# Bidirectional SSM states stored block-first, new limits and prices in a hand planner, and three loads and products moved

## The chip, the core and the metric

The program runs on one core of a Trainium2 chip. The core has TensorE (matmuls into PSUM, its weight loads are listed apart as PEld), VectorE (DVE in the profile), ScalarE (ACT), GpSimd (POOL) and SyncE (SP, which here only issues DMAs). Each engine works through its own queue in order. The metric is the device time of one execution in microseconds (us); lower is better.

## The reference

One layer of an encoder, for 256 tokens of 2048 features, all in float32. Shortened:

```python
h = rmsnorm(x, norm_mix_pre)
q_na, k_na, v_na, u_ssm, q_mem = split(h @ w_in)          # 1024,1024,1024,512,512
y_na  = neighbourhood_attention(q_na, k_na, v_na, na_rpb)  # 8 heads of 128
y_ssm = s5_mixer(u_ssm, ...)                               # 32 groups of 16 channels
y_mem = memory_cross_attention(q_mem, mem, ...)            # 4 heads of 128, 256 memory tokens
y = concat(rmsnorm(y_na), rmsnorm(y_ssm), rmsnorm(y_mem))
x = x + rmsnorm(y @ w_out, norm_mix_post)
f = square(relu(rmsnorm(x, norm_mlp_pre) @ w_ff1)) @ w_ff2
x = x + rmsnorm(f, norm_mlp_post)
```

The part that matters here is `s5_mixer`: for each of two directions and 32 groups, a complex diagonal recurrence of 64 states over the tokens, `h[t] = lam_bar * h[t-1] + b_bar @ u[t]`, then `y = Re(c @ h)`, summed over both directions, plus `d*u`, then GELU and a gate.

## The kernel before

**The weights set the pace.** All weight matrices are cut in 128x128 blocks and laid out in the order of use, eight blocks to a chunk `128x1024` (372 loads in all, the first chunk in three pieces). SP loads a chunk into `wraw`; ScalarE rounds it to `wh` (`conv_high`), VectorE makes the rest `wl = wraw - wh` (`conv_low`), and TensorE multiplies in three passes, high by high, high by low and low by high (`mm3`, `mm_tok`), which keeps float32 accuracy at the fast rate. `take` hands out blocks; when a chunk is used up it converts the chunk two ahead (`AHEAD`) and calls `tick`. `wraw`, `wh` and `wl` have three buffers each.

**A planner written by hand.** The order of instructions on each engine is the program's order. Everything beside the weight stream (attention heads, the SSM, norms) is written as generators, `spawn`ed with a priority and the engines that they load (`uses`). Four clocks in `clk` (V, G, A for VectorE, GpSimd, ScalarE, and E for TensorE) are moved on by a price for every instruction issued (`Engine.call`, `book`). `tick` lets a task take its next step if its time has come and if each engine in `uses` is booked ahead of TensorE by less than `BACK`, in ns. Nothing of this runs on the chip: it decides only in which order instructions stand in the queues.

**The SSM.** Tokens are permuted so that a block is four consecutive tokens, 64 blocks (`NB`). `prep_b` builds input weights, `incr` multiplies them with the inputs and ScalarE copies the result into `XS[g]` (two halves g of the states, each 128 partitions x 2 (real, imaginary) x 16 x 64 blocks; the backward direction is written in reverse). `tree` then runs a prefix scan over the 64 blocks in place: six levels up, five down. On a level with distance h it takes every 2h-th block `dst` and the one h before it, `src`, and does `dst += a*src` for complex a in four VectorE instructions of `2*16*n` elements, n being 32, 16, 8, 4, 2, 1 going up and 1, 3, 7, 15, 31 going down. `ssm_out` multiplies the finished states with output weights: 128 matmuls with 32 stationary columns each, four side by side, whose moving operand `h` is one state row of 63 or 64 blocks.

**Loads.** `load_b` fetches the raw SSM input weights; k-th blocks of x come through `x_in`. `before_dma[c]` holds calls to be made just before chunk c is loaded.

**The end of the first half.** The last quarter of the output projection is evacuated, its squares are summed, `rsqrt_pool` takes a power on GpSimd with a refining step on VectorE, `gpost[3]` (norm weights of the last quarter) is multiplied in by GpSimd, and `x1_part` adds the result to x, 128 columns at a time first, so that TensorE can transpose (`h_turn`) and go on with the MLP.

Of the kernel before, what the change touches and what calls it, by code (L numbers as in the profile page):

```python
# [11 lines left out]
F32 = mybir.dt.float32  # L12
# [27 lines left out]
MARGIN1 = 1200.0  # L40
SH_V = 1e9
SH_G = 500.0
BACK_V, BACK_G, BACK_A = 2600.0, 4000.0, 2200.0
WARM0, WARM1 = 7, 10
LAM_BACK = 900.0
GLU_AT = 1
# [55 lines left out]
def hybrid_kernel(ctx: ExitStack, tc: tile.TileContext, A: dict, out: bass.AP, dbg=None):  # L102
# [16 lines left out]
    class Engine:  # L119
# [3 lines left out]
        def __getattr__(self, name):  # L123
            f = getattr(self.raw, name)
            e = self.e

            def call(o, *a, **kw):
                n = 1
                for d in o.shape[1:]:
                    n *= d  # L130
                if e == "E":
                    m = a[0].shape[-1]
                    if name == "transpose":
                        c = 110.0
                    elif a[0].dtype == F32R:
                        c = n * 0.4225
                    else:
                        c = max(n, 128) * 1.69 * (0.31 if m == 32 else 1.0) if n > 4 else 110.0
                elif name == "tensor_reduce":
                    c = 80 + 1.04 * a[0].shape[1] * a[0].shape[2]  # L140
                elif e == "A":
                    c = 100 + 0.83 * n + (95 if any(isinstance(x, bass.AP) for x in kw.values()) else 0)
                elif e == "V":
                    c = (72 if n > 64 else 140) + n * {"tensor_copy": 0.52, "reciprocal": 8.0, "tensor_tensor_scan": 1.04,
                                   "tensor_scalar": 0.76, "memset": 0.3}.get(name, 1.04)
                else:
                    c = 155 + n * {"tensor_scalar": 0.9, "memset": 0.0, "tensor_copy": 1.6}.get(name, 2.1)
                book(e, c)
                return f(o, *a, **kw)  # L149
            return call  # L150
# [17 lines left out]
    def tt(eng, o, a, b, op):  # L168
        eng.tensor_tensor(o, a, b, op=op)
# [10 lines left out]
    def act(o, i, f=AF.Copy, **kw):  # L180
        ACT.activation(o, i, f, **kw)
# [37 lines left out]


    tasks = []
    BACK = dict(V=BACK_V, G=BACK_G, A=BACK_A)

    def spawn(gen, pri=1, uses="VA", after=None):
        i = sum(1 for t in tasks if t[0] <= pri)
        tasks.insert(i, [pri, gen, clk[after] + MARGIN + MARGIN1 if after else clk["E"], uses])
        return gen
# [15 lines left out]
    def tick():  # L243
        for t in list(tasks):
            more = t[2] <= clk["E"]
            while more and all(clk[e] - clk["E"] < BACK[e] for e in t[3]):
                more = step(t)

    def drain(g):
# [179 lines left out]
    def x_in(k0, k1):  # L429
        q = k0 // 8  # L430
        if q not in xst:
            xst[q] = a2.tile([128, 8, 256], F32, name="xst", tag="AB", bufs=2)
        nc.sync.dma_start(xst[q][:, k0 - 8 * q:k1 - 8 * q, :], A["xT"][:, k0:k1, :])

    def m_in(q):
        mst[q] = a1.tile([128, 4, 256], F32, name="mst", tag="xst", bufs=2)
# [214 lines left out]
    def prep_b(ut):  # L651
        yield from until(lambda: ut in loaded and clk["E"] > loaded[ut][1])
        raw = loaded[ut][0]
        w = a2.tile([128, 2, 2, 4, 4, 16], F32, name="W", tag="W", bufs=1)
        par = a2.tile([128, 4, 2, 2, 4], F32, name="par", tag="par", bufs=1)
        for i, x in enumerate((cfr, cfi, lbr, lbi)):
            act(par[:, i], x[:, 8 * ut:8 * ut + 8].rearrange("p (d q) -> p d q", d=2)[:, :, None, :]
                .to_broadcast([128, 2, 2, 4]))
        for l in range(4):
            o = w[:, :, :, :, l, :]  # L660
            src = (w[:, :, :, :, l - 1, :].rearrange("p d c q b -> p (d c q) b") if l
                   else raw.rearrange("p (n b) -> p n b", b=16))
            r_, i_ = (par[:, 2 * min(l, 1) + i].rearrange("p d c q -> p (d c q)")[:, :, None].to_broadcast([128, 16, 16])
                      for i in range(2))
            t = a2.tile([128, 2, 2, 4, 16], F32, name="pt", tag="pt", bufs=1)
            tt(V, t.rearrange("p d c q b -> p (d c q) b"), src, i_, mult)
            tt(V, o.rearrange("p d c q b -> p (d c q) b"), src, r_, mult)
            tt(V, o[:, :, 0], o[:, :, 0], t[:, :, 1], sub)
            tt(V, o[:, :, 1], o[:, :, 1], t[:, :, 0], add)
            yield True  # L670
        yield
        act(W0[ut].rearrange("p d c q j b -> p (d c q) j b"),
            w[:, :, :, :, 0, :].rearrange("p d c q b -> p (d c q) b")[:, :, None, :].to_broadcast([128, 16, 2, 16]))
        w0_done.add(ut)
        if ut % 2 == 0:
            XS[ut // 2] = a2.tile([128, 2, 16, NB], F32, name="XS", tag="AB", bufs=2)
        for d in range(2):
            for j in range(2):
                h = slice(64 * j, 64 * j + 64)
                act(wx[h, :, ::-1 if d == 0 else 1, j, :], w[h, d].rearrange("p c q l b -> p (c q) l b"))  # L680
            yield
            wt = a2.tile([128, 2, 4, 128], F32, name="W1T", tag="W1T", bufs=2)
            for c in range(2):
                p = att()
                for q in range(4):
                    PE.transpose(p[:, q * 128:(q + 1) * 128], wx[:, 4 * c + q].rearrange("p l j b -> p (l j b)"), ident)
                act(wt[:, c].rearrange("p q m -> p (q m)"), p)
            spawn(incr(ut, d, wt), 2, "A")
            yield
        yield from until(lambda: (ut, 1) in xs_part)  # L690

    def incr(ut, d, wt):

        yield from until(lambda: ssm_done and (d == 0 or (ut, 0) in xs_part))
        p = att()
        X = p.rearrange("p (c q m) -> p c q m", c=2, q=4)
        for c in range(2):
            for q in range(4):
                PE.matmul(X[:, c, q, :], wt[:, c, q, :], U4[:, 4 * ut + q, :], start=True, stop=True,
                          skip_group_check=True)  # L700
        c0 = 8 * (ut % 2) + 4 * d
        o = XS[ut // 2][:, :, c0:c0 + 4, :]
        act(o[:, :, :, ::-1] if d else o, X)
        xs_part.add((ut, d))
        yield

# [45 lines left out]
    def tree(g):  # L752

        X = XS[g]
        cols = slice(16 * g, 16 * g + 16)
        for up, l in [(1, l) for l in range(LEV)] + [(0, l) for l in range(LEV - 2, -1, -1)]:
            h = 1 << l
            d0 = 2 * h - 1 if up else 3 * h - 1
            n = len(range(d0, NB, 2 * h))
            dst, src = X[:, :, :, d0::2 * h], X[:, :, :, d0 - h:NB - h:2 * h]  # L760
            t = a2.tile([128, 2, 16, NB // 2], F32, name="ps", tag="ps", bufs=1)[:, :, :, 0:n]
            tt(V, t, src[:, ::-1], pw[:, l, 0:2, cols][:, :, :, None].to_broadcast([128, 2, 16, n]), mult)
            tt(V, dst, dst, t, add)
            tt(V, t, src, pw[:, l, 2, cols][:, None, :, None].to_broadcast([128, 2, 16, n]), mult)
            tt(V, dst, dst, t, add)
            yield True
        yield
# [4 lines left out]
    def ssm_out(ut):  # L772
# [7 lines left out]
        for i in range(4):  # L780
            for d in range(2):
                l = (i + 1) % 4 if d == 0 else (4 - i) % 4
                for c in range(2):
                    for q in range(4):
                        h = H[:, c, 8 * (ut % 2) + 4 * d + q, :]

                        if d == 0:
                            o0, h = (1, h[:, 0:NB - 1]) if l else (0, h)
                        else:
                            o0, h = (0, h[:, NB - 2::-1]) if l else (0, h[:, ::-1])  # L790
                        n = NB - 1 if l else NB
                        PE.matmul(p[32 * q:32 * q + 32, i * NB + o0:i * NB + o0 + n], CC[ut][:, l, c, 4 * d + q, :],
                                  h, start=False, stop=(i == 3 and d == 1 and c == 1), skip_group_check=True,
                                  tile_position=(0, 32 * q))
# [113 lines left out]


    for ut in range(2):  # L910
        load_b(ut)
    spawn(lam_task("V"), 2, "V")
    spawn(b_task(), 3, "VA")
    spawn(c_task(), 3, "VA")
    spawn(k0_task(), 3, "VA")
    spawn(tree_task(), 4, "V")
    st = spawn(ssm_task(), 5, "GA")

    st_rx = {}
# [284 lines left out]
    ts(v1, v1, 1.0 / D, mult, EPS, add)  # L1204
    stt(v1[:, 1:2], sx, 1.0 / D, v1[:, 1:2], mult, add)
    rsqrt_pool(r1, v1)
    for t in range(2):
        a = acc1[:, t, quarter(3)]
        tt(G, a, a, gpost[3], mult)
    B = ExitStack()  # L1210
    bp = B.enter_context(tc.tile_pool(name="bp", bufs=1, side="right"))
    hs = bp.tile([128, KT, 2, 256], F32R, name="hs")
# [38 lines left out]
    x1_part(slice(128, 256))  # L1251
    h_turn(1)
    h_high(1)
    conv_low(first)
    W.nv += 1
    h_low(0)
# [236 lines left out]
```

## Time and profile before

| | us |
|---|---|
| median of 3 runs | 1175.65 (1172.53 to 1177.12) |
| the profiled execution | 1176.17 |
| its span, first to last instruction | 1174.4 |

The span falls into stages: 0 to 58 us the first projections, 58 to 150 memory keys and values, 150 to 336 neighbourhood attention with the SSM's trees beside it, 336 to 440 the output projection, 440 to 454 the norm between the halves, and from 454 the MLP, in which TensorE is never idle until 1150. In a row of the timeline stand start, duration, engine, line, operation, `out<-in`, shapes, count, and in brackets how long the engine was idle before it and who ended that. Since one helper issues nearly all instructions, all have line 149 and are told apart by their tiles.

### The profile page before, as it was taken

What the parts mean: (1) busy time and instruction counts of PE and PEld (TensorE: products, weight loads), DVE (VectorE), ACT (ScalarE), POOL (GpSimd) and SP (SyncE); (2) the same over time, 40 slices, a digit from 0 to 9 for tenths busy, and PEclk for the clock granted to TensorE, in tenths of its full rate; (3) what the DMA queues carried; (4) which work ended last, traced back from release to release, by engine and by line L of the source; (5) the groups of instructions that cost most, each with busy time, mean ns of one, the idle gap of its engine ahead of it and who ended that gap; (6) DMA issues with size and microseconds to landing.
All of it is one profiled execution on the core that took longest, in us unless ns stands there. A gap on an engine that the chain in (4) does not pass through costs nothing.

```text
span 1174.4 us, 17404 instructions
## 1 busy us (share of the span) xinstructions
PE 1129.9 (96%) x6776; PEld 976.4 (83%) x6776; DVE 718.5 (61%) x1060; ACT 588.7 (50%) x908; POOL 97.7 (8%) x161
## 2 busy tenths in 40 slices
PE   8989896999989998999999999999999999999996
PEld 7978796989878887888888888888888888888885
DVE  6767498566966766676665444445666665445454
ACT  5677643566455546555455434343444544344342
POOL 1750000010000034000000000000000000011011
PEclk9999998999999999999999999999999999999998
DMA  8875353344444684666666666666666666666673
GB/s 285 303 218 171 109 162 104 100 131 138 154 127 142 187 280 145 182 190 188 195 187 189 186 191 184 191 185 192 189 190 194 186 192 184 193 193 197 189 210 127
DMA packets 62723, 213.05 MB, mean 181 GB/s; under 512 B 7216, under 2 KB 8752, under 8 KB 62640
## 3 DMA queue, kind: packets, MB, share of 16 engines
q1 hardware_dynamic: 62352, 211.84, 58.6%
q8 instruction: 53, 0.87, 0.3%
q14 instruction: 30, 0.25, 0.1%
q10 hardware_dynamic: 288, 0.09, 0.0%
HBM read 209.81 MB, written 2.10 MB: 180 GB/s over the span
## 4 chain that ended last, share of the span: by engine, by line
PE 72%; DVE 3%; issue 1%; ACT 1%; POOL 0%; DVEq 0%; ACTq 0%; POOLq 0%
PE acc L149 66%; PE big L149 5%; PE att L149 2%; DVE wl L149 1%; DVE ps L149 1%; DVE XS L149 1%; POOL x L149 0%; DVE facc L149 0%; ACT CC L149 0%; ACT wh L149 0%; DVE mn L149 0%; DVE rt L149 0%; DVE P L149 0%; DVE r L149 0%; ACT yH L149 0%
## 5 line engine op out<-in xcount | busy, mean ns | idle before, releaser
L149 DVE TENSOR_TENSOR wl<-wraw,wh 128x1024 fp32r<-128x1024 f32 (+1 forms) x372 | 454.2, 1225 | 389.2 <-ACT wh L149 389.0
L149 ACT ACTIVATE wh<-wraw 128x1024 fp32r<-128x1024 f32 (+1 forms) x372 | 391.2, 1054 | 419.4 <-PE acc L149 303.5
L149 PE MATMUL acc<-hs,wh 128*128 128x512 f32 (+1 forms) x996 | 346.4, 391 | 0.0
L149 PE MATMUL acc<-hs,wl 128*128 128x256 f32 x992 | 279.8, 283 | 0.0
L149 PEld LDWEIGHTS acc<-hs,wh 128*128 128x128 f32 x996 | 187.1, 188 | 38.6 <-ACT hs L149 0.2
L149 PEld LDWEIGHTS acc<-hs,wl 128*128 128x128 f32 x992 | 187.9, 190 | 0.0
L149 PE MATMUL acc<-wh,fH 128*128 128x512 f32 x448 | 178.8, 399 | 0.0
L149 PE MATMUL acc<-wh,fL 128*128 128x512 f32 x448 | 176.7, 394 | 0.0
L149 PE MATMUL acc<-wl,fH 128*128 128x512 f32 x448 | 175.7, 392 | 0.0
L149 PEld LDWEIGHTS acc<-wh,fL 128*128 128x128 f32 x448 | 84.1, 188 | 21.8
L149 PEld LDWEIGHTS acc<-wl,fH 128*128 128x128 f32 x448 | 84.1, 188 | 20.1
L149 PEld LDWEIGHTS acc<-wh,fH 128*128 128x128 f32 x448 | 84.1, 188 | 19.2
L149 PE MATMUL acc<-xH,wl 128*128 128x256 f32 x256 | 74.8, 292 | 9.3 <-DVE wl L149 9.2
L149 PE MATMUL acc<-xH,wh 128*128 128x256 f32 x256 | 77.2, 301 | 4.4 <-ACT wh L149 4.4
L149 PE MATMUL acc<-xL,wh 128*128 128x256 f32 x256 | 74.0, 289 | 0.0
L149 PEld LDWEIGHTS acc<-xH,wl 128*128 128x128 f32 x256 | 50.6, 198 | 10.6 <-DVE wl L149 10.6
L149 PEld LDWEIGHTS acc<-xH,wh 128*128 128x128 f32 x256 | 50.8, 199 | 5.2 <-ACT wh L149 4.6
L149 PEld LDWEIGHTS acc<-xL,wh 128*128 128x128 f32 x256 | 50.7, 198 | 0.4
L149 POOL TENSOR_TENSOR facc<-facc,g 128x512 f32<-128x512 f32 x6 | 10.1, 1710 | 475.5 <-DMA g<-in_g_dram 475.5
L149 PE MATMUL acc<-wh,mixn 128*128 128x512 f32 x128 | 40.8, 396 | 0.0
L149 ACT ACTIVATE P<-P,mn 128x256 f32<-128x256 f32 x24 | 12.0, 501 | 40.8 <-DVE mn L149 40.8
L149 DVE TENSOR_TENSOR XS<-XS,ps 128x32 f32<-128x32 f32 (+9 forms) x44 | 29.1, 661 | 1.5
(305 smaller groups left out, 1503.0 us busy)
## 6 DMA issues: line engine op xcount, KB each, us to landing
wraw<-in_w_dram SPq DMA_DIRECT2D x369, 512.0 KB, 4.3
tokst<-in_xt_dram SPq DMA_DIRECT2D x4, 512.0 KB, 7.9
mst<-in_memT_dram SPq DMA_DIRECT2D x4, 512.0 KB, 4.6
tokst<-in_mt_dram SPq DMA_DIRECT2D x4, 512.0 KB, 6.3
bias<-in_bias_dram SPq DMA_DIRECT2D x8, 256.0 KB, 4.0
x<-in_xt_dram SPq DMA_DIRECT2D x8, 256.0 KB, 5.9
out_dram<-facc SPq DMA_DIRECT2D x8, 256.0 KB, 2.4
xst<-in_xT_dram SPq DMA_DIRECT2D x7, 256.0 KB, 7.4
```

Source lines behind the costliest of these rows:

```text
L149: return f(o, *a, **kw)
```

## The change

Five things are edited.

1. `XS` and the tree's scratch `ps` are stored with the block as outer axis and the 2x16 state columns inside. `incr`, `tree` and `ssm_out` index them accordingly; what is computed stays the same.
2. The tree task is let in by a limit of its own, key `v`: VectorE's bookings less than 1700 ns ahead of TensorE, where it was 2600 as for others.
3. ScalarE's price for n elements goes from `100 + 0.83n` (and 95 if any operand beside the input is a tile) to `205 + 0.83n`, plus 80 with a tile as scale or with a bias, plus 186 with an accumulated sum; its limit goes from 2200 to 3800 ns.
4. The loads of the first two blocks of SSM input weights move from the start of SP's queue to just before chunks 5 and 6, and the first block of x is issued by ScalarE's queue in place of SP's.
5. The two GpSimd products with `gpost[3]` stand, in the program, behind the first two transposes and roundings of the next stage.

```diff
-BACK_V, BACK_G, BACK_A = 2600.0, 4000.0, 2200.0
+BACK_V, BACK_G, BACK_A, BACK_TREE = 2600.0, 4000.0, 3800.0, 1700.0
...
-                    c = 100 + 0.83 * n + (95 if any(isinstance(x, bass.AP) for x in kw.values()) else 0)
+                    c = (205 + 0.83 * n + (80 if isinstance(kw.get("scale"), bass.AP) or "bias" in kw else 0)
+                         + (186 if "accum_out" in kw else 0))
...
-    BACK = dict(V=BACK_V, G=BACK_G, A=BACK_A)
+    BACK = dict(V=BACK_V, G=BACK_G, A=BACK_A, v=BACK_TREE)
...
-            while more and all(clk[e] - clk["E"] < BACK[e] for e in t[3]):
+            while more and all(clk[e.upper()] - clk["E"] < BACK[e] for e in t[3]):
...
-        nc.sync.dma_start(xst[q][:, k0 - 8 * q:k1 - 8 * q, :], A["xT"][:, k0:k1, :])
+        (nc.sync if k0 else nc.scalar).dma_start(xst[q][:, k0 - 8 * q:k1 - 8 * q, :], A["xT"][:, k0:k1, :])
...
-            XS[ut // 2] = a2.tile([128, 2, 16, NB], F32, name="XS", tag="AB", bufs=2)
+            XS[ut // 2] = a2.tile([128, NB, 2, 16], F32, name="XS", tag="AB", bufs=2)
...
-        o = XS[ut // 2][:, :, c0:c0 + 4, :]
-        act(o[:, :, :, ::-1] if d else o, X)
+        act(XS[ut // 2][:, ::-1 if d else 1, :, c0:c0 + 4], X.rearrange("p c q m -> p m c q"))
...
-            dst, src = X[:, :, :, d0::2 * h], X[:, :, :, d0 - h:NB - h:2 * h]
-            t = a2.tile([128, 2, 16, NB // 2], F32, name="ps", tag="ps", bufs=1)[:, :, :, 0:n]
-            tt(V, t, src[:, ::-1], pw[:, l, 0:2, cols][:, :, :, None].to_broadcast([128, 2, 16, n]), mult)
+            dst, src = X[:, d0::2 * h], X[:, d0 - h:NB - h:2 * h]
+            t = a2.tile([128, NB // 2, 2, 16], F32, name="ps", tag="ps", bufs=1)[:, 0:n]
+            tt(V, t, src[:, :, ::-1], pw[:, l, 0:2, cols][:, None].to_broadcast([128, n, 2, 16]), mult)
             tt(V, dst, dst, t, add)
-            tt(V, t, src, pw[:, l, 2, cols][:, None, :, None].to_broadcast([128, 2, 16, n]), mult)
+            tt(V, t, src, pw[:, l, 2, cols][:, None, None, :].to_broadcast([128, n, 2, 16]), mult)
             tt(V, dst, dst, t, add)
...
-                        h = H[:, c, 8 * (ut % 2) + 4 * d + q, :]
+                        h = H[:, :, c, 8 * (ut % 2) + 4 * d + q]
...
-        load_b(ut)
+        at(before_dma, 5 + ut, load_b, ut)
...
-    spawn(tree_task(), 4, "V")
+    spawn(tree_task(), 4, "v")
...
     rsqrt_pool(r1, v1)
-    for t in range(2):
-        a = acc1[:, t, quarter(3)]
-        tt(G, a, a, gpost[3], mult)
...
     x1_part(slice(128, 256))
     h_turn(1)
     h_high(1)
+    for t in range(2):
+        a = acc1[:, t, quarter(3)]
+        tt(G, a, a, gpost[3], mult)
     conv_low(first)
```

## The prediction

> **What bounds the kernel now.** I read the page first (TensorE busy, the chain), then busy time by stage, then the list of who waited for whom, then the timeline around each wait of TensorE, and last the groups by form.
>
> ```profile
> PE 1129.9 (96%) x6776; PEld 976.4 (83%) x6776; DVE 718.5 (61%) x1060; ACT 588.7 (50%) x908; POOL 97.7 (8%) x161
> ```
>
> TensorE is busy in 1129.9 of 1174.4 us. A change that leaves its matmuls alone can only win from the 44.5 us in which it is idle, so the question is where these lie. Stages (columns: stretch, its length, then busy us of PE, PEld, DVE, ACT, POOL):
>
> ```profile
> 58.00:150.00 92.00, 84.57 (x549) 72.40 (x548) 60.69 (x125) 64.92 (x126) 17.56 (x53) 0.98 0.53 160
> 150.00:200.00 50.00, 39.59 (x300) 37.92 (x299) 48.33 (x73) 23.10 (x39) 0.73 (x1) 0.92 0.41 127
> 285.00:336.00 51.00, 45.54 (x328) 43.01 (x325) 49.10 (x69) 22.12 (x42) 0.74 (x1) 0.97 0.44 146
> 440.00:454.00 14.00, 10.46 (x60) 8.88 (x60) 10.83 (x17) 8.16 (x15) 8.56 (x7) 0.88 0.34 108
> ```
>
> The reader is to see the second and third row: 10.4 and 5.5 us of TensorE idle, and VectorE at 48.3 of 50 and 49.1 of 51 us. These are the two prefix trees of the SSM (one per half of the states). There VectorE is the bound: TensorE needs `wl`, the low half of each weight chunk, from the same VectorE queue. Its waits, one by one (in brackets the idle time before and who ended it):
>
> ```profile
> 156.49 0.38 PE L149 MATMUL acc<-xH,wl 128*128 128x256 f32 x1 [1.11 <-DVE wl L149]
> 177.96 0.32 PE L149 MATMUL att<-U,W1T 128*128 128x64 f32 x1 [1.31 <-ACT W1T L149]
> 193.84 0.58 PE L149 MATMUL acc<-xH,wh 128*128 128x256 f32 x1 [4.36 <-ACT wh L149]
> 198.27 0.58 PE L149 MATMUL acc<-xH,wl 128*128 128x256 f32 x1 [3.64 <-DVE wl L149]
> 317.39 0.39 PE L149 MATMUL acc<-xH,wl 128*128 128x256 f32 x1 [0.93 <-DVE wl L149]
> 325.15 0.54 PE L149 MATMUL acc<-xH,wl 128*128 128x256 f32 x1 [3.33 <-DVE wl L149]
> 333.52 0.50 PE L149 MATMUL acc<-wl,mixm 128*128 128x512 f32 x1 [0.93 <-DVE wl L149]
> ```
>
> The 4.36 us at 193.84 are put down to ScalarE, but ScalarE was busy in only 23 of these 50 us: its queue stood behind a softmax step that waited for VectorE. So 8.0 us at the end of tree one and 5.2 us in tree two are VectorE's backlog.
>
> **The tree's layout.** Level l of a tree takes every 2·2^l-th block. In the old layout the block is the innermost axis, so elements lie 8 bytes apart on level 0, 16 and more above. Groups of VectorE by form, 150 to 345 us (count, busy us, mean ns):
>
> ```profile
> L149 DVE TENSOR_TENSOR qk<-acc,rb_x 128x512 f32<-128x512 f32 x8 | 5.5, 688 | 0.2 <-PE acc L149 0.2
> L149 DVE TENSOR_TENSOR XS<-XS,ps 128x1024 f32<-128x1024 f32 x4 | 4.9, 1226 | 0.1
> L149 DVE TENSOR_TENSOR XS<-XS,ps 128x512 f32<-128x512 f32 x4 | 4.4, 1107 | 0.1
> L149 DVE TENSOR_TENSOR ps<-XS,pw 128x512 f32<-128x512 f32 x4 | 4.3, 1084 | 0.1
> L149 DVE TENSOR_TENSOR XS<-XS,ps 128x480 f32<-128x480 f32 x4 | 4.2, 1045 | 0.1
> L149 DVE TENSOR_TENSOR ps<-XS,pw 128x480 f32<-128x480 f32 x4 | 4.1, 1028 | 0.1
> L149 DVE TENSOR_TENSOR XS<-XS,ps 128x256 f32<-128x256 f32 x4 | 2.6, 658 | 0.1
> L149 DVE TENSOR_TENSOR ps<-XS,pw 128x256 f32<-128x256 f32 x4 | 2.6, 645 | 0.1
> L149 DVE TENSOR_TENSOR W<-W,par 128x256 f32<-128x256 f32 x6 | 2.5, 418 | 0.0
> L149 DVE TENSOR_TENSOR XS<-XS,ps 128x224 f32<-128x224 f32 x4 | 2.4, 588 | 0.1
> L149 DVE TENSOR_TENSOR ps<-XS,pw 128x224 f32<-128x224 f32 x4 | 2.3, 576 | 0.1
> ```
>
> A contiguous 512 takes 688 ns and a contiguous 256 takes 418; the tree's take 1107 and 658. The 1024 (8-byte steps) costs nothing extra. In the new layout the innermost 32 (or twice 16) lie together on every level, so I give each form the contiguous time: 688; 654 for 480 and 384 for 224, on the line through 256 and 512; 418. Saved over both trees, four instructions of each row: (1107+1084-2·688)·4 = 3.26, (1045+1028-2·654)·4 = 3.06, (658+645-2·418)·4 = 1.87, (588+576-2·384)·4 = 1.58, in all 9.8 us; forms of 128 and fewer at nothing. That is **4.9 us for each tree**. In tree one all of it falls in VectorE's unbroken run that ends in the 8.0 us of waits, so TensorE gets 4.9. In tree two the waits come step by step, and what has been saved ahead of each covers all but 0.3 us of the 5.2: 4.9 again. What is late next is the rest: 3.1 us at the end of tree one, and the 1.31 us on ScalarE.
>
> The planner's own price for VectorE (72 ns and 1.04 per element, 604 for 512) does not change; it was 0.5 us short of each strided 512, which is how it let in more stages than VectorE could carry, and is nearly right for contiguous ones. The lower backlog limit (1700 for 2600 ns) holds a stage back by at most 0.9 us. Behind it wait only the SSM outputs; in front go the `wl`. It could win up to the 3.1 us left; below, a later second tree could lose as much as it is held back, 0.9. I take 0.
>
> **Readers and writers of the states.** ScalarE's eight evacuations (512 elements) now read PSUM 256 bytes apart and write runs of four. No row shows ScalarE so; by VectorE's extra of (1107-688)/512 = 0.8 to (658-418)/256 = 0.9 ns per element they cost 0 to 8·512·0.9 = 3.7 us of an engine with half its time free. I take 0, because ScalarE ends only 1.31 us of waits here. The four `ssm_out` blocks read their moving operand 128 bytes apart instead of contiguously:
>
> ```profile
> 219.56 1.97 PE L149 MATMUL att<-XS,CC 128*32 128x63 f32 x128
> 164.89 0.28 PE L149 MATMUL acc<-xH,wh 128*128 128x256 f32 x1
> 165.01 0.28 PE L149 MATMUL acc<-xL,wh 128*128 128x256 f32 x1
> ```
>
> 128 matmuls in 1.97 us, less some 0.2 for the last one's drain, are 32 groups of four column tiles at 55 ns, 0.86 ns per column. Elsewhere TensorE takes 256 columns of 4 bytes each 0.12 us, 0.47 ns per column. So a tile here reads at little over half the rate it can; a halving by the stride would just be hidden. Bounds: 0, and 0.9 ns for every column of 128 groups, 128·64·0.9 = 7.4 us. I take 0, nearest to the 0.47 row. The Trainium skill (Advanced Engine Details and Errata, section Memory Cachelines) speaks against the change: SBUF lines have 16 bytes and two hits on each are needed for full speed, PSUM's have 8. VectorE's rows agree (8-byte steps free, 16-byte steps not); no run yet shows it for TensorE, and by that rule the 7.4 us would be lost.
>
> **ScalarE's prices.**
>
> ```profile
> L149 ACT ACTIVATE U<-uT 32x256 f32<-32x256 f32 x16 | 6.6, 414 | 0.2
> 136.28 0.33 PE L149 MATMUL att<-CC,W 128*32 128x96 f32 x5 [2.53 <-issue]
> 265.59 0.31 PE L149 MATMUL att<-CC,W 128*32 128x96 f32 x4 [2.35 <-ACT CC L149]
> ```
>
> A copy of 256 was booked at 100+0.83·256 = 312 ns and takes 414; now 417 is booked. So steps that TensorE takes up behind ScalarE were put in its queue too early: both `CC` waits above. Right prices could win both, 2.53+2.35 = 4.9 us. Against that the limit rises from 2200 ns, seven such copies or 2.9 us real, to 3800, nine or 3.7: a queue up to 0.8 us deeper ahead of a `wh`. That bites where ScalarE is fullest, from 58 to 150 us (64.9 of 92). TensorE's idle time there, 92-84.6 = 7.4 us, is 4.9 without the first `CC` wait; as the upper end I let it double. No row tells which of the two wins, and they are alike in size: I take 0 and keep -4.9 and +4.9.
>
> **The start.**
>
> ```profile
> 0.72 0.86 SPq L648 DMA_DIRECT2D W<-in_b_dram  x2
> 1.63 0.42 SPq L433 DMA_DIRECT2D xst<-in_xT_dram  x1
> 2.49 0.35 ACTq L197 DMA_DIRECT2D lam<-in_lam_dram  x1
> 4.86 0.51 ACT L149 ACTIVATE xH<-xst,vecs 128x256 fp32r<-128x256 f32 x1 [2.17 <-DMA xst<-in_xT_dram]
> 26.41 0.38 PE L149 MATMUL big<-xH,wh 128*128 128x256 f32 x1 [0.42 <-ACT wh L149]
> ```
>
> Three issues leave the head of SP's queue (the weights follow at about 1.63+0.42 = 2.05, so they start 1.3 us earlier, at 0.72). But the first `xT` block now stands behind `lam` in ScalarE's queue: issued at 2.49+0.35 = 2.84, not 1.63, so `xH` starts 1.2 us later, and TensorE with it. Neither lasts: at 26.41 TensorE waits for weights that come through a DMA queue with the same bytes ahead of them, the two SSM loads now before chunks 5 and 6. Those loads are needed only after GpSimd's lambda chain. I take 0, between -1.3 and +1.2.
>
> **The last norm weights.**
>
> ```profile
> 441.24 0.16 DVE L149 TENSOR_TENSOR rt<-ry 128x2 f32<-128x2 f32 x1 [0.84 <-POOL ry L149]
> 441.31 2.48 POOL L149 TENSOR_TENSOR acc<-acc,gpost 128x512 f32<-128x512 f32 x2
> 441.44 1.15 DVE L149 SCALAR_TENSOR_TENSOR rt<-rt,v 128x2 f32<-128x2 f32 x1
> 442.62 1.19 DVE L149 SCALAR_TENSOR_TENSOR r<-rt,ry 128x2 f32<-128x2 f32 x1
> 444.25 0.33 PE L149 MATMUL att<-ident,x 128*128 128x128 f32 x1 [2.94 <-DVE x L149]
> ```
>
> Two 2-element steps take 1.15 and 1.19 us instead of 0.16, each until one of GpSimd's two products ends; TensorE waits behind them. Moving the products out of the way would win 2.0 us. But between the old and new place in the program lie no GpSimd instructions and nothing that writes what the products read: GpSimd still takes them up right after its power at 441.3. I take 0; -2.0 if the new place adds a wait that holds them, and up to +2.5 (their length) if they then hold back `wl`.
>
> **Sum.** 1176.2 (span 1174.4 and 1.8 around it) - 4.9 - 4.9 = **1166.4 us**. The profiled execution lies 0.5 above the median 1175.65, so this counts as 0.8% faster than before. About 0.5%, 5.9 us, is what a measurement of this kernel tells from no change: faster means under 1169.8, slower over 1181.5.
>
> **Rivals.**
> 1. What I left at 0 comes too: both `CC` waits (-4.9) or one of them with the norm weights (-2.4-2.0): about 1161.7. For it: the waits are there and their cause is a price. Against: the unmoved place in GpSimd's queue. Chance 0.18.
> 2. Strided moving reads cost VectorE's 0.9 ns per column: +7.4, 1173.8. For it: the same step costs VectorE that much. Against: the 0.47 row. Chance 0.15. (The Trainium skill's Memory Cachelines, above, give this one.)
> 3. ScalarE's deeper queue becomes the wait: up to +4.9, 1171.3, astride the border. For it: ScalarE's 71% in that stage. Against: its prices are now right. Chance 0.15.
> 4. Slower: in `ssm_out` the four tiles of a group now read four neighbouring floats at a time. If such reads are served one after another, a group takes 4·55 = 220 ns, 165 more; 128·165 ns = +21.1, 1187.5. The gain is eaten from 9.8 us/128 = 77 ns more (132 ns a group), and the time is slower from 15.1 us/128 = 118 ns more (173 ns a group). Against: the four tiles run side by side now. Chance 0.08.
> 5. The change does not do what it says: patterns with runs of 16 cost VectorE what strides did, 1176. Chance 0.04.
>
> Forecast: 0.40. Faster: forecast, rival 1 and half of 3, 0.65; same: 2, 5, half of 3, 0.27; slower: 4, 0.08. The range goes from rival 1 with some start gain, 1158, to rival 5, 1177; it leaves out rival 4 and the edge of 1.
>
> **What would show it.** Right: tree forms of 512 near 688 ns; TensorE idle in the two tree stretches down to about 5.5 and 0.6; `ssm_out` blocks still 1.97 us; the two 2-element steps at 441 still over 1 us. Wrong: `ssm_out` at 3.8 us or 7 us; new waits for `wh` between 60 and 100 us; TensorE's first weights matmul far beyond 7 us with 26.41 shifted as well.

## The result, and the profile after

| | us | ratio to the kernel before |
|---|---|---|
| before, median in the same comparison | 1176.11 | |
| changed, median of 6 | 1181.87 | 1.0053 (95%: 1.0033 to 1.0074) |
| changed, profiled execution | 1182.86 (span 1181.1) | |

The change makes the kernel slower by half a per cent, about 6.2 us. The prediction, 1166.4 with a range up to 1177, is wrong, in the sign too. The engines' line on the page of the changed kernel:

```profile
PE 1145.4 (97%) x6776; PEld 991.5 (84%) x6776; DVE 709.8 (60%) x1060; ACT 588.6 (50%) x908; POOL 98.4 (8%) x161
```

TensorE is idle for 1181.1 - 1145.4 = 35.7 us, 8.8 less than before; VectorE has 8.7 us less to do. So far this is what was forecast. But the same 6776 matmuls now keep TensorE busy for 15.5 us more. The stages of the changed kernel (stretch, length, busy us of PE, PEld, DVE, ACT, POOL, then the granted clock, DMA share, GB/s):

```profile
58.00:150.00 92.00, 89.86 (x604) 78.20 (x603) 61.69 (x124) 70.14 (x136) 19.77 (x57) 1.00 0.58 178
150.00:200.00 50.00, 45.62 (x336) 43.82 (x335) 42.14 (x85) 27.93 (x56) 1.49 (x2) 0.93 0.42 129
285.00:336.00 51.00, 47.77 (x330) 44.31 (x330) 42.57 (x70) 22.22 (x42) 2.14 (x2) 0.97 0.55 166
440.00:454.00 14.00, 11.00 (x69) 9.71 (x68) 9.44 (x19) 6.22 (x17) 9.23 (x9) 0.92 0.47 154
```

VectorE is no longer full in the tree stretches (42 of 50 us), and TensorE's idle time there falls from 10.4 to 4.4 and from 5.5 to 3.2; from 58 to 150 us it falls from 7.4 to 2.1. The tree itself, VectorE's groups by form from 150 to 345 us in the changed kernel (count, busy us, mean ns):

```profile
L150 DVE TENSOR_TENSOR XS<-XS,ps 128x512 f32<-128x512 f32 x4 | 3.2, 805 | 0.1
L150 DVE TENSOR_TENSOR ps<-XS,pw 128x512 f32<-128x512 f32 x4 | 2.7, 686 | 0.1
L150 DVE TENSOR_TENSOR ps<-XS,pw 128x480 f32<-128x480 f32 x4 | 2.6, 654 | 0.1
L150 DVE TENSOR_TENSOR XS<-XS,ps 128x256 f32<-128x256 f32 x4 | 1.7, 426 | 0.1
L150 DVE TENSOR_TENSOR ps<-XS,pw 128x224 f32<-128x224 f32 x4 | 1.5, 386 | 0.1
```

These are the contiguous prices but for the first row. Three of its four take 0.69 us like the others; the fourth takes 1.14, beside an instruction of GpSimd:

```profile
168.17 0.73 POOL L150 TENSOR_TENSOR sum_mo<-sum_mo,sq 128x256 f32<-128x256 f32 x1 [88.07 <-ACT sq L150]
168.30 1.14 DVE L150 TENSOR_TENSOR XS<-XS,ps 128x512 f32<-128x512 f32 x1
```

Now the reader of the states, TensorE's group of the four `ssm_out` blocks in the stretch from 200 to 380 us, first in the kernel before, then in the changed one:

```profile
L149 PE MATMUL att<-XS,CC 128*32 128x63 f32 (+1 forms) x512 | 7.9, 219 | 0.0
```

```profile
L150 PE MATMUL att<-XS,CC 128*32 128x63 f32 (+1 forms) x512 | 21.0, 348 | 0.0
```

13.1 of the 15.5 us are here. A block takes 5.14 to 5.41 us where it took 1.97, the third for instance:

```profile
339.68 5.14 PE L150 MATMUL att<-XS,CC 128*32 128x63 f32 x128
```

The start, a timeline of the changed kernel (start, duration, engine, line, operation, in brackets the idle time before and who ended it):

```profile
2.88 0.45 ACTq L434 DMA_DIRECT2D xst<-in_xT_dram  x1
9.35 0.51 ACT L150 ACTIVATE xH<-xst,vecs 128x256 fp32r<-128x256 f32 x1 [6.66 <-DMA xst<-in_xT_dram]
10.21 0.58 PE L150 MATMUL big<-xH,wh 128*128 128x256 f32 x1 [4.36 <-ACT wh L150]
11.74 0.33 SPq L300 DMA_DIRECT2D wraw<-in_w_dram  x1
```

The first block of `xT`, issued at 2.88, is used only at 9.35, and TensorE's first weights matmul stands at 10.21. The next chunk is asked for only at 11.74 (7.66 in the kernel before), when a buffer comes free: the weight stream itself is late. And waits of TensorE, from the same trace. The kernel before doesn't have them; only the third, right behind the second tree, has a counterpart there, of 0.93:

```profile
184.21 0.95 PE L150 MATMUL att<-ident,P 128*128 128x128 f32 x4 [2.74 <-ACT P L150]
216.63 3.67 PE L150 MATMUL att<-U,W1T 128*128 128x64 f32 x16 [2.95 <-ACT W1T L150]
328.32 0.50 PE L150 MATMUL acc<-wl,mixm 128*128 128x512 f32 x1 [2.41 <-DVE wl L150]
378.03 0.49 PE L150 MATMUL acc<-wh,mixn 128*128 128x512 f32 x1 [2.10 <-ACT wh L150]
```

So three things have to be told apart: what the strided reads cost and why, what the late start costs, and what the planner's edits win or lose. Experiments are given as ratios to the kernel before on the same chip; a ratio of 0.001 is 1.2 us.

### The profile page after: what moved, and what is told of

The parts are those of the page before. It is cut to its first block, busy times and chain, and to the rows that moved or that the text cites. A ratio compares the mean times of both kernels' runs of the same rounds, so it can differ in the third digit from the quotient of the medians.

```text
span 1181.1 us, 17405 instructions
## 1 busy us (share of the span) xinstructions
PE 1145.4 (97%) x6776; PEld 991.5 (84%) x6776; DVE 709.8 (60%) x1060; ACT 588.6 (50%) x908; POOL 98.4 (8%) x161
## 4 chain that ended last, share of the span: by engine, by line
PE 84%; DVE 4%; ACT 4%; issue 3%; POOL 3%; DMA 2%; DVEq 0%; SPq 0%; ACTq 0%; POOLq 0%
PE acc L150 73%; PE att L150 6%; PE big L150 5%; DVE wl L150 2%; ACT wh L150 1%; DMA wraw<-in_w_dram 1%; DVE ps L150 1%; DMA xst<-in_xT_dram 1%; ACT P L150 0%; POOL cs L150 0%; POOL u L150 0%; POOL x L150 0%; DVE XS L150 0%; POOL t L150 0%; DVE rt L150 0%
## 5 line engine op out<-in xcount | busy, mean ns | idle before, releaser
L150 PEld LDWEIGHTS acc<-wh,mixn 128*128 128x128 f32 x128 | 24.7, 193 | 8.3 <-ACT wh L150 2.5
L150 DVE SCALAR_TENSOR_TENSOR ff<-fr 128x256 f32<-128x256 f32 x64 | 27.2, 425 | 2.2
```

## Which reads are slow

Three probes take the changed kernel and let each of the four blocks read other places of the state tile. `o` is the first element of tile q (four tiles run side by side), `st` the step from column to column, in floats. What the blocks read is no longer what the layer needs, so only the rows of the blocks are used, not the time of these runs. The expectations count a block from its first to its last start; a row of the timeline is 0.2 to 0.4 us longer, by the last matmul's own time.

**Probe 1.** Steps of 4, 8, 16 and 128 bytes, tiles apart.

```diff
-                        h = H[:, :, c, 8 * (ut % 2) + 4 * d + q]
+                        X = H.rearrange("p m c s -> p (m c s)")
+                        o, st = [(64 * q, 1), (128 * q, 2), (256 * q, 4), (4 * q, 32)][ut]
+                        h = X[:, o:o + (NB - 1) * st + 1:st]
```

> The changed kernel, but the four output blocks read other places of the state tile (so the SSM's output is not the layer's): block 1 steps of 4 bytes, block 2 steps of 8, block 3 steps of 16 with the four column tiles 1 KB apart, block 4 steps of 128 with the four tiles 16 bytes apart. Unchanged they take about 5.0 us each, 1.97 before the change. Theory A, a moving read pays for each new 16-byte line: blocks 1 and 2 take 1.97, blocks 3 and 4 some 3.8 to 5.0. Theory B, the cost comes from four tiles reading one line at once: blocks 3 and 4 take 1.97 too. Theory C, any step but 1 is slow: block 1 alone is fast.

The four blocks in its timeline, in this order:

```profile
227.31 1.99 PE L150 MATMUL att<-XS,CC 128*32 128x63 f32 x128
241.78 2.12 PE L150 MATMUL att<-XS,CC 128*32 128x63 f32 x128
332.96 3.96 PE L150 MATMUL att<-XS,CC 128*32 128x63 f32 x128
349.64 3.71 PE L150 MATMUL att<-XS,CC 128*32 128x63 f32 x128
```

Steps of 8 bytes are nearly free, steps of 16 bytes double the block. The last block has the changed kernel's step of 128 bytes, but its four tiles lie 16 bytes apart instead of 4, and it takes 3.71, not 5.2. So there are two costs, one of the step and one of where the tiles lie.

**Probe 2.** `o, st = [(512 * q, 8), (512 * q, 3), (q, 4), (0, 32)][ut]`: 32 and 12 bytes with tiles 2 KB apart, 16 bytes on neighbouring floats, and 128 bytes with all four tiles on the same floats.

> The changed kernel, whose four blocks of C H read other places of the state tile, so that the output isn't the reference's. In the earlier probe a block took 1.77 us with steps of 4 bytes, 1.90 with 8, 3.66 with 16 and tiles 1 KB apart, 3.43 with 128 and tiles 16 bytes apart, against 4.8 to 5.2 in the changed kernel (128 bytes, tiles 4 bytes apart). Now: steps of 32 bytes and tiles 2 KB apart; 12 bytes, 2 KB apart; 16 bytes, tiles 4 bytes apart; 128 bytes, all four tiles at the same address. If a column that lies on a new group of 16 bytes costs double: 3.4 to 3.7; 2.8 to 3.3 (three of four columns are on a new one); and if four tiles on one group wait for each other, 4.8 to 5.2 for the third and the fourth. If only different tiles on a power of two wait for each other: 3.5 and 1.8 to 2.0 for the first two. If tiles that ask for the same address are served at once: 3.4 to 3.7 for the fourth.

```profile
225.97 4.03 PE L150 MATMUL att<-XS,CC 128*32 128x63 f32 x128
242.48 3.02 PE L150 MATMUL att<-XS,CC 128*32 128x63 f32 x128
334.92 3.96 PE L150 MATMUL att<-XS,CC 128*32 128x63 f32 x128
351.60 5.75 PE L150 MATMUL att<-XS,CC 128*32 128x63 f32 x128
```

The first two came close to what the first theory had. With steps of 12 bytes three of four columns begin in a new group of 16 bytes, with 8 bytes one of two, from 16 bytes on every one, and start to start the blocks take 2.77, 1.90 and 3.66 to 3.73: about 3.7 us times that share, and never under 1.8. The third was expected at 4.8 to 5.2 and is 3.66: four tiles on one group of 16 bytes do not wait for each other by that alone. The fourth (5.39) excludes that equal addresses are served at once.

**Probe 3** tells what is left: long steps on a shared group, or that all columns of all tiles lie at one place of a period of 128 bytes. `o, st = [(q, 20), (q, 16), ((q // 2) * 4 + q % 2, 32), (q, 28)][ut]`: 80, 64, 128 and 112 bytes; on neighbouring floats but for the third, where two tiles lie in one group and two in the next.

> The changed kernel, whose four blocks of C H read other places of the state tile, so that the output isn't the reference's: steps of 80 bytes, tiles 4 bytes apart; 64 bytes, tiles 4 bytes apart; 128 bytes, two tiles on one group of 16 bytes and two on the next; 112 bytes, tiles 4 bytes apart. If the last third of the cost comes from all columns lying at the same place of a period of 128 bytes: 3.4 to 3.8; more than that, 3.8 to 5 (two places of the period); 3.4 to 4.5; 3.4 to 3.8. If it comes from long steps on a shared group: 4.8 to 5.4 for the first and the last, too. If the period is 64 bytes: 3.4 to 3.8, 4.8 to 5.4, 3.4 to 4.5, 3.4 to 3.8.

```profile
224.69 4.21 PE L150 MATMUL att<-XS,CC 128*32 128x63 f32 x128
241.38 4.02 PE L150 MATMUL att<-XS,CC 128*32 128x63 f32 x128
334.49 4.13 PE L150 MATMUL att<-XS,CC 128*32 128x63 f32 x128
351.33 3.94 PE L150 MATMUL att<-XS,CC 128*32 128x63 f32 x128
```

All four are back at the doubled time (start to start 3.91, 3.72, 3.84 and 3.64; the first is a little over what was expected, the second a little under). Long steps on a shared group (the first and the last) aren't the cause, nor is a period of 64 bytes (the second). Two places of 128 bytes (the second, the third) are enough to take the extra away. Only where every read of all four tiles falls on one place of a 128-byte period, as in the changed kernel, does a block take over 5 us. Only steps of 128 bytes show it here; longer ones were not tried, and what part of the memory that place is, the runs don't say.

So the changed kernel pays twice: about 2.0 us per block for the step (3.96 for 1.99), 8.0 in all, and about 1.3 for the shared place (5.14 to 5.41 for 4.0), 5.1 in all, together the 13.1 us of the two group rows.

## What each part is worth

**The layout alone** (the kernel before with the `XS`, `ps`, `incr`, `tree` and `ssm_out` lines of the diff).

> The kernel before with the new layout of states and scratch alone. Theory A (the strided reads of the output blocks cost 3.2 us each, 12.7 in all, and the trees win their 9.8 or less): 1176.1 + 12.7 - 9.8 = 1179 or somewhat more, with four output blocks of 5 us. Rival (the loss sits in the start and in the planner's new order, and the long output blocks only fill time in which TensorE would have waited): 1166 to 1172.

Ratio 1.0017 (1.0005 to 1.003). Its blocks take 5.23 to 5.55 us, and TensorE's idle time in the two tree stretches is 5.66 and 2.77: what the tree wins, the reads take.

**Everything but the layout** (the changed kernel with the old layout).

> The changed kernel with the old layout, everything else of the change kept. Theory A: output blocks back at 1.97 us (-12.7), the trees slow again (at most +9.8), so 1181.9 - 12.7 + 5 to 9.8 = 1174 to 1179. Rival (the loss sits in start and order): 1182 or more, since the trees' gain is lost as well.

Ratio 0.9995 (0.9984 to 1.0006). The other edits together are worth nothing, although their waits for `P`, `W1T` and at the output projection are all there. The parts don't add up: on the new layout the same edits cost 1.0053 - 1.0017 = 0.0036, 4.2 us (some 2.8 either way).

**Another layout: real and imaginary part innermost.** TensorE then steps 8 bytes, and VectorE reads pairs. First on the changed kernel (`incr` and `tree` index the tile accordingly):

```diff
-            XS[ut // 2] = a2.tile([128, NB, 2, 16], F32, name="XS", tag="AB", bufs=2)
+            XS[ut // 2] = a2.tile([128, 16, NB, 2], F32, name="XS", tag="AB", bufs=2)
...
-                        h = H[:, :, c, 8 * (ut % 2) + 4 * d + q]
+                        h = H[:, 8 * (ut % 2) + 4 * d + q, :, c]
```

> The changed kernel with a third layout: 16 state columns outside, then the block, then the real and imaginary part innermost. The output blocks read in steps of 8 bytes, and the trees take pairs of 8 bytes that lie 16 bytes and more apart. Theory A: output blocks 1.97 us, tree forms of 512 near 690 ns if two hits on a line are enough, so 1181.9 - 12.7 = 1169; if VectorE pays by the jump and not by the element, about 900 ns for 512 and some 1174. Rival C (any step is slow): output blocks stay at 5 us, 1182.

Ratio 0.9947 (0.9929 to 0.9964), 12.5 us less than the changed kernel (some 3 either way), by this alone. The blocks take 2.11 to 2.13 us.

**The same layout on the kernel before, nothing else changed.**

> The same layout on the kernel before, with nothing else changed: beside the same with GpSimd's norm products really moved, 1167.64. That one shows waits of TensorE for x, released by GpSimd, of 0.92, 4.02 and 0.74 us, where the others have one of 3.0: if the real move costs these 2.7 us, 1164 to 1166; if it costs nothing, 1167 to 1168. By the sum of the layout alone (1.7) and the strided reads (12.7): 1163.5.

Median 1165.41, ratio 0.9926 (0.9911 to 0.9942): faster than both kernels, and near what I had forecast for the change. By its ratio it is the fastest version here; two more below (0.9928 and 0.9935) can't be told from it. Its tree stretches:

```profile
150.00:200.00 50.00, 44.31 (x334) 43.19 (x333) 43.71 (x76) 24.58 (x40) 0.73 (x1) 0.93 0.43 149
285.00:336.00 51.00, 48.17 (x445) 44.59 (x445) 41.07 (x70) 25.92 (x50) 2.90 (x3) 1.00 0.51 164
```

TensorE is idle for 5.7 and 2.8 us of them. A faster tree without slow reads is worth 0.0074, 8.7 us; the slow reads cost 1.0017 - 0.9926 = 0.0091, 10.7 us, with some 2 us of uncertainty beside the 13.1 of the rows.

## The late start

**The changed kernel with the first `xT` load back on SP's queue.**

> The changed kernel with the first xT load back on SP's queue, everything else as changed. In the changed kernel's trace that load is issued on ScalarE's queue at 2.88 us and lands at 9.26, and the first weights matmul stands at 10.21 behind a wait of 4.36 us for wh; its weights matmuls are 4.5 us behind those of the kernel before at the start, 1.8 at 54 us and 1.3 at 73. If the start is caught up later, as I forecast: no wait over 1 us at the first weights matmul, and a time within 0.7 us of the changed kernel's 1181.9. If the delay that is left at 73 us stays to the end: 1.3 to 1.8 us less, 1180.1 to 1180.6. If all of the first wait reaches the end: 4.4 less, 1177.5.

```profile
3.28 0.51 ACT L150 ACTIVATE xH<-xst,vecs 128x256 fp32r<-128x256 f32 x1 [0.59 <-DMA vecs<-in_vecs_dram]
5.51 0.56 PE L150 MATMUL big<-xH,wh 128*128 128x256 f32 x1
```

`xH` starts at 3.28 and the first weights matmul at 5.51, with no wait ahead. Median 1177.93, ratio 1.0025 (1.0015 to 1.0035) where the changed kernel has 1.0053: about 0.0028, 3.3 us, but by the two intervals anything from 0.6 to 6, which leaves room for the last two of the three expectations. The traces are sharper. The first weights matmul lies 4.7 us ahead of the changed kernel's (5.51 and 10.21), the four matmuls on `P` 2.85 (181.36 and 184.21), the matmul behind the wait of 2.10 us 2.65 (375.38 and 378.03), and the first matmul on `x` at the end of the first half 2.65 (448.38 and 451.03). So over half of the delay is never caught up.

**The pair layout on the changed kernel, with the same load back.**

> The changed kernel with real and imaginary part innermost and with the first xT load back on SP's queue. Without the second it has 0.9947 of the kernel before; the same layout on the old planner and loads has 0.9926; the xT load alone was worth 0.0028 on the changed layout (1.0053 to 1.0025). If the load is all that the other edits cost: 0.991 to 0.993, 1163 to 1165. If the planner's edits cost something of their own: 0.994 or more, 1166 and above.

Ratio 0.9935 (0.992 to 0.995), between the two expectations. With the pair layout the planner's and the load edits cost 0.9947 - 0.9926 = 0.0021; the load's part is 0.0012, about half, but these intervals don't tell half from none or all. In the two traces TensorE's first matmul on `x` stands at 434.96 and, with the load back, 432.85.

## The planner's edits

**ScalarE's prices and limit on the kernel before** (with the moved norm products, which change nothing there).

> The kernel before with ScalarE's new prices and its limit of 3800 and with the last norm weights moved: the old layout, the old limit for the tree, the old loads. If ScalarE's edits are what empties the stretch from 58 to 150 us (idle 7.43 before, 2.14 in the changed kernel): its idle time there falls to 2 or 3 us and the time is 1169 to 1172 on a scale where the kernel before has 1174.5. If the waits that came with the changed kernel (P, W1T and wl at 184, 217 and 328 us, and wh and wl at the GLU) are ScalarE's work being priced higher and so let in later: these waits, 2.7, 2.9, 2.4 and 2.9 us, are here too and give the gain back, 1174 to 1178. If they come from the tree's lower limit or the moved loads, none of them is here. The moved norm weights by themselves: 0, as the changed kernel's row of rt and its gap of 3.00 us show.

Ratio 0.9974 (0.9962 to 0.9986). The idle time from 58 to 150 us falls from 7.4 to 2.1, as in the changed kernel, so this edit is what empties that stage. But part comes back; two waits of its trace:

```profile
183.84 1.54 PE L150 MATMUL att<-U,W1T 128*128 128x64 f32 x6 [5.31 <-ACT W1T L150]
367.31 0.79 PE L150 MATMUL acc<-wh,mixn 128*128 128x512 f32 x1 [2.10 <-ACT wh L150]
```

**The layout with the tree's lower limit.**

> The kernel before with the new layout and the tree's lower limit of 1700, and ScalarE's old prices, old loads. Beside it stands the layout alone, 1.7 us over the kernel before (ratio 1.0017). If the lower limit is worth nothing, as I forecast: the same, 1175 to 1177. If it lets the tree in so late that the SSM's output is ready too late for the GLU (2.10 and 0.77 us of waits at 378 us in the changed kernel, and 5 us of delay gathered there): these waits are here and the time is 1179 to 1182. If ScalarE's prices do that: the waits are not here.

Ratio 1.006 (1.0047 to 1.0074), 5 us over the layout alone. My mechanism for it fell: at the output projection there is only a wait of 0.76. The tree begins at 159 us instead of 147, the last step of the second tree starts at 328 instead of 323, and the wait behind it grows. That wait, and the clock after it:

```profile
330.11 0.79 PE L149 MATMUL acc<-wl,mixm 128*128 128x512 f32 x1 [3.39 <-DVE wl L149]
```

```profile
330.00:332.00 2.00, 1.89 (x5) 1.51 (x6) 2.00 (x4) 0.00 (x0) 0.00 (x0) 0.50 0.44 109
332.00:336.00 4.00, 4.00 (x11) 3.12 (x10) 1.00 (x2) 2.38 (x5) 0.00 (x0) 0.50 0.81 264
```

3.39 us where the layout alone waits 2.44, and then six us at a granted clock of 0.50. Behind the wait of the layout alone the clock stays at 1.00:

```profile
325.33 0.50 PE L149 MATMUL acc<-wl,mixm 128*128 128x512 f32 x1 [2.44 <-DVE wl L149]
```

```profile
326.00:330.00 4.00, 4.00 (x20) 3.34 (x19) 3.60 (x5) 1.59 (x5) 0.75 (x1) 1.00 0.78 229
```

The longer wait and half of the six us are some 4 of the 5 us, an estimate from one trace of each.

**The changed kernel with the old limit for the tree.**

> The changed kernel with the tree's limit back at VectorE's 2600, all else as changed. The layout with the lower limit took 5.8 us more than the layout alone, its first tree beginning at 159 us instead of 147. If that limit is what lets the tree end late in the changed kernel (its first tree runs from 159 to 217 us, 58 us, against 45 in the kernel before): the tree begins before 150 us, ends before 200, and the time is 1174 to 1178, 4 to 8 less than the changed kernel's 1181.9. If ScalarE's higher prices stretch the tree by themselves (its waits at 177, 184 and 217 us are ScalarE's): the tree still ends after 210 and the time is 1180 to 1183.

Ratio 1.0054 (1.0035 to 1.0072), no different from the changed kernel (to some 3 us), though the last step of the first tree now starts at 201 us instead of 217. So with ScalarE's new prices no price of the limit shows, nor one of the late end of the first tree.

**ScalarE's prices with the pair layout.**

> The kernel before with two things alone: the state tile with real and imaginary part innermost, and ScalarE's new prices and limit. The tree's limit, the loads and the norm weights are those before. If the parts add up: 1174.5, less 12.7 for the strided reads, plus 1.7 for the layout, less 3.1 for ScalarE's prices: about 1160.5, between 1159 and 1163. If ScalarE's prices only fill the waits that the faster tree removes: 1163 to 1166.

Ratio 0.9928 (0.9906 to 0.9949), the same as without them (0.9926). The gain of 0.0026 on the old layout does not add to the faster tree. The idle time from 58 to 150 us is 2.1 here and 6.4 without, from 150 to 200 it is 7.8 and 5.7, and TensorE is busy for 1130.0 and 1126.3 us: what one stage wins comes back in later ones.

**Why idle time that goes doesn't all become time.** Sixteen matmuls `U,W1T` in the timeline of the kernel before, after a wait of 1.31 us:

```profile
177.96 2.00 PE L149 MATMUL att<-U,W1T 128*128 128x64 f32 x16 [1.31 <-ACT W1T L149]
```

In the changed kernel the same sixteen, at 216.63 above, take 3.67 us after a wait of 2.95. The changed kernel by stretches around that wait; the third number from the end is the granted clock:

```profile
213.00:216.00 3.00, 0.68 (x6) 0.47 (x5) 2.97 (x4) 2.33 (x9) 0.00 (x0) 1.00 0.84 306
217.00:219.00 2.00, 2.00 (x11) 2.00 (x11) 1.97 (x3) 1.01 (x2) 0.84 (x1) 0.50 0.00 0
219.00:221.00 2.00, 2.00 (x11) 2.00 (x11) 1.10 (x2) 0.65 (x2) 0.00 (x0) 0.50 0.00 0
221.00:223.00 2.00, 2.00 (x12) 2.00 (x11) 0.00 (x0) 1.08 (x2) 0.00 (x0) 0.50 0.82 240
223.00:226.00 3.00, 3.00 (x26) 3.00 (x26) 0.69 (x1) 2.37 (x5) 0.00 (x0) 0.97 0.06 20
```

For six us TensorE counts as fully busy at half the clock. The wait of 2.95 us costs about three more behind it (half of the six, an estimate), which no row of idle time shows. The new waits for `P` and `W1T` and at the output projection are of that length, the `CC` waits that went too. Between the two kernels this evens out: the mean granted clock of their profiled executions is 0.987 before and 0.988 after. So the clock doesn't explain the 6.2 us.

## The norm weights

**The pair layout on the kernel before, with the two products where GpSimd really takes them up later** (in the program behind the last `x1_part`, columns 256 to 511).

> The kernel before with its own planner and loads, the state tile laid out with real and imaginary part innermost (TensorE steps 8 bytes instead of 128, VectorE reads pairs), and GpSimd's two last norm products really behind the products of the second quarter. If the strided reads are the whole loss of the changed layout: the four blocks of C H fall to about 1.9 us each, 12 us less than with the changed layout alone, 1163.5 to 1165 on a scale where the kernel before has 1174.5. If the moved products are also worth the two waits of VectorE and the 3 us gap at 448 us, 1 to 2 us less, 1161.5 to 1163. If the gain of the pair layout in the changed kernel (13.7 us) came with the changed planner: 1168 or more.

Median 1167.64, ratio 0.9937 (0.9924 to 0.9949), against 0.9926 without; the intervals overlap. Its waits for `x` and the products:

```profile
429.12 1.11 PE L149 MATMUL att<-ident,x 128*128 128x128 f32 x4 [0.92 <-DVE x L149]
432.61 4.51 POOL L149 TENSOR_TENSOR acc<-acc,gpost 128x512 f32<-128x512 f32 x2
439.38 0.48 PE L149 MATMUL att<-ident,x 128*128 128x128 f32 x1 [4.02 <-POOL x L149]
440.60 0.48 PE L149 MATMUL att<-ident,x 128*128 128x128 f32 x1 [0.74 <-POOL x L149]
```

The first wait shrinks from 2.88 to 0.92, but the products, now beside VectorE's work, take 4.51 us, and TensorE waits 4.76 us for the `x` behind them. Whether that costs time is open; no gain shows.

## Why the prediction was wrong, by its steps

**The tree's layout: right.** The forms cost what the contiguous rows said, and the gain was put at 9.8 us; with pairs, so without the slow reads, it is 8.7 (6.8 to 10.5). There the first tree stretch fell from 10.4 to 5.7 us of idle, as forecast (5.5), the second only to 2.8 instead of 0.6: of its waits one of 2.4 us behind the tree remained. So 7.4 us of the 9.8 came where they were forecast, and the close sum is in part luck.

**Readers of the states: this step failed.** "I take 0, nearest to the 0.47 row." The trace of before showed a tile reading at little over half TensorE's rate, and I argued that a halving by the stride would just be hidden. Slack of two there was: steps of 8 bytes cost next to nothing. But from 16 bytes on every column begins in a new group of 16 bytes, four times as many groups as in contiguous reads and not twice, and that doubles a block. The 0.47 row belongs to contiguous reads by one tile over all columns and says nothing of four tiles' strided reads; the nearest row on strides was VectorE's own, 0.9 ns per column, and by it rival 2 had 7.4 us for the step, measured 8.0. Rival 4 had the second mechanism, tiles in each other's way, at 21.1 us; it is 5.1, and by one place of 128 bytes, not by neighbouring floats as such. The rivals were weighed one against the other, but both happened, and 13.1 us lie above the 9.8 that the tree wins. The Trainium skill, Advanced Engine Details and Errata, section Memory Cachelines, says that at least two accesses must fall on each 16-byte line of SBUF for full speed. The probes bear it out for TensorE's moving reads: 8-byte steps 2.12 us against 1.99, 16-byte steps 3.96.

**The start: this step failed too.** "Neither lasts": taken as 0 between -1.3 and +1.2, it is about +3.3 by the ratios and 2.65 in the traces at the end of the first half. I moved the load by the 1.2 us of its issue. But a load on ScalarE's queue is not ahead of what SP has queued: ScalarE could use it 6.5 us after its issue. In the changed kernel's trace the loads of both queues land in the order of their issue: SP's of 2.58 us at 8.86, ScalarE's of 2.88 at 9.26, SP's of 3.40 at 9.66. And the delay isn't absorbed where I said: the next chunk loads are issued later (11.74; the 22nd at 56.5 us, and at 54.2 with the load back on SP's queue). And in the kernel before, from its first weights matmul to 58 us, TensorE waits only 2.4 us for weights (0.43, 0.76, 0.42 and 0.76), less than the delay of 4.5 that was to go into such waits. The Trainium skill, DMA: Bandwidth & Descriptors, section Issuing engines are not separate DMA queues, says that DMAs of different engines run on the same 16 DMA engines and interleave; the order in which these loads land agrees.

**ScalarE's prices: 0 was right for the sum, for another reason.** Both ends were there: the stage from 58 to 150 us lost 5.3 us of idle time (the `CC` wait among it), and new waits of ScalarE's came between 177 and 217 us and at the output projection. On the old layout 3.1 us remain as gain, with a faster tree none; why it is lost there stays open.

**The tree's limit: mis-sized.** Held to 0.9 us of loss, it cost 5 (some 2 either way) with ScalarE's old prices and nothing that shows with the new ones; a stage held back moves the whole tree, here by 12 us.

**ScalarE's evacuations and the norm weights: right.** The evacuations of the states take 587 ns where they took 595. GpSimd still takes the products up right behind its power, and VectorE's two steps stand as before, in the changed kernel's timeline:

```profile
447.89 2.48 POOL L150 TENSOR_TENSOR acc<-acc,gpost 128x512 f32<-128x512 f32 x2
447.96 1.21 DVE L150 TENSOR_TENSOR rt<-ry 128x2 f32<-128x2 f32 x1 [0.84 <-POOL ry L150]
449.21 1.19 DVE L150 SCALAR_TENSOR_TENSOR rt<-rt,v 128x2 f32<-128x2 f32 x1
```

**The sum by the runs,** step by step from the kernel before to the changed one: -8.7 for the tree (pairs), +10.7 for the slow reads (the layout alone), +0.9 for the planner's edits and the other loads and products (1.0025 - 1.0017), +3.3 for the start, in all the 6.2 us. The 0.9 is within what the intervals leave. In another order the steps have other sizes, since with the old layout all the other edits come to nothing.

## What to carry to other kernels

A layout has more than one reader. Before data is turned for the engine that reads it most, price every other reader at the new step, with the nearest row of a strided read on any engine; a layout between the two (here pairs innermost, 8 bytes for TensorE, runs of pairs for VectorE) may give each what it needs. A load that the first matmul waits for must be issued first, not merely on another queue. And look behind a wait of TensorE of over two us for a slow stretch, which can cost as much again: here one of 2.95 us had it, one of 2.44 had not.

## What was not expected of the hardware

- TensorE's moving reads: four column tiles side by side take 1.99 us for 128 matmuls of 63 or 64 columns with 4-byte steps, 2.12 with 8, 3.02 with 12, 3.7 to 4.2 from 16 bytes on, and 5.1 to 5.8 when all reads of all tiles fall on one place of a 128-byte period. Neighbouring floats at other steps cost nothing more (16 bytes: 3.96, like tiles far apart).
- After a wait of 2.95 us TensorE had a granted clock of 0.50 for six us, after one of 1.31 it stayed at 1.00, and after one of 2.44 in the run of the layout alone too; after 2.10 and 0.77 us close together at 378 us it lay at 0.54 to 0.60 for four.
- VectorE's pairs (8 bytes, then a step) run at the contiguous rate: 690 to 698 ns for 512 in the pair layout on the kernel before, where single floats at steps of 16 bytes and more took 1084 to 1107.
- A VectorE instruction of 512 elements took 1.14 us beside an instruction of GpSimd that ran for 0.6 us of it, and 0.69 without.
